# Strassen's method for the layer-1 projections of a two-layer streaming encoder step

## The chip, the cores and the metric

The kernel runs on one core of one Trainium2 chip. The metric is device time in microseconds (us) for one execution of the whole program. The engines are named as in the profile: PE is TensorE with its matmuls (PEld are its weight loads), DVE is VectorE, ACT is ScalarE, POOL is GpSimd, and SP is SyncE, which here issues the DMAs. SBUF is the on-chip memory, PSUM the accumulation memory that PE writes.

## The reference, cut to what matters

A model of two layers (width 1024) takes 512 prompt rows and 32 sample rows. The kernel handles them together as T = 544 columns of a transposed activation matrix. Layer 0 is RWKV-7 time mixing, layer 1 differential attention. The change concerns the input projection of layer 1, its gating, and the output projection that follows:

```python
def diff_layer(x, mk, mv, k_past, v_past, layer_idx, norm_w, w_out, w_in, ...):
    h = rmsnorm(x, norm_w)
    q, k, v, qm, gate = jnp.split(h @ w_in, [MIX_W, 2 * MIX_W, 3 * MIX_W, 3 * MIX_W + MEM_W], axis=-1)
    ...                                     # 12 heads of 128: softmax(q1 k1) - lam * softmax(q2 k2), times v
    y_mem = mem_attention(qm, mk, mv)       # 4 heads of 128 over 256 memory rows
    out = jnp.concatenate([o.reshape(B, T, MIX_W).astype(x.dtype), y_mem], axis=-1) * jax.nn.silu(gate)
    return x + out @ w_out, k, v
```

`w_in` has 1024 rows and 7168 columns: 12 blocks of 128 columns each for q, k and v, 4 for qm and 16 for the gate, 56 blocks in all. All data is float32.

## The kernel before

**Precision scheme.** PE multiplies in a reduced format (`F32R`). Every operand is therefore held as a high part and a low part (`hh`, `hl` for the activations, `whi`, `wlo` for the weights), and a product is three matmuls: high by high, high by low, low by high.

**A projection.** `proj` (L244) computes one block of 128 output columns for all 544 columns. `weights` (L216) loads the block in two halves of 128 x 512 (`raw`, five buffers, L206), casts each half on ACT (L224, `whi`) and subtracts on DVE (L225, `wlo`). Each of `whi` and `wlo` has two buffers that hold a whole block. `gemm` (L228) then runs, for each half of 272 columns, 8 steps over the contraction with three matmuls each (L239 to L241), 48 matmuls in all, into one of the three PSUM banks of `psg`. The caller's `evac` takes the result out of PSUM.

**Order.** The program is written with a tile framework that orders the instructions of each engine ahead of time from priorities and an estimate of durations, and puts in all semaphores. At run time each engine works through its list in order, so an instruction that waits holds up all those behind it.

**Layer 1** (`layer1` L1038, `diff_group` L1111, `mem_head` L782) goes through three groups of four heads. Each head has three projections, k, q and v, whose evacuations write `k`, `qp` (L1141, L1142) and `v`. POOL makes the low part `kz` of the keys (L1152), and the attention of the head follows: score matmuls (L1185 to L1187), maximum on DVE (L776), exponential on ACT (L777), `combine` on DVE (L1250 to L1252), transposes and the product with v (L1193, L1198). After the four heads come the 32 sample rows of the group, and four gate projections (`gate`, L682), each multiplied with the head's output into a tile `og` of SBUF (L1244). Two memory heads follow each of the first two groups, with a projection for qm, attention and a projection for the gate. PE's list mixes the projections of the next head with the attention of the present one.

**Before and after layer 1.** `w_out` (L847) of layer 0 loads sixteen gated tiles from DRAM (`os`, L856), splits each into `hi` and `lo` (L858, L859) and multiplies with the output weights. Its sum `x1` stays in SBUF. The norm of layer 1 scales it into `hn` (L1031), ACT casts `hh` (L1033) and POOL subtracts `hl` (L1034), while PE computes memory values (`mem_kv`, L747). `w_out` of layer 1 finds its sixteen gated tiles `og` in SBUF, splits them, and adds into `x1` (L1097) before the last norm.

Of the kernel before, what the change touches and what calls it, by code (L numbers as in the profile page):

```python
# [8 lines left out]
F32 = mybir.dt.float32  # L9
# [4 lines left out]
ALU = mybir.AluOpType  # L14
# [31 lines left out]
OSB = 4  # L46
ANCH = ('endd',)
# [8 lines left out]
class Trunk:  # L56
# [187 lines left out]
    def proj(self, src, c0, evac):  # L244
        self.gemm([self.weights(src, c0)], [(self.hh, self.hl)], evac)

# [447 lines left out]
    def dest(self, g, sg):  # L694

        return self.o1[g] if self.o1 else sg

    def put(self, g, t):
        if not self.o1:
            self.nc.sync.dma_start(self.oscr[g // 8][:, g % 8, :], t[:])  # L700
# [81 lines left out]
    def mem_head(self, i, h, w, cq, cg, p):  # L782
# [16 lines left out]
        self.proj(w, cq + h * P, lambda ps, v: nc.scalar.mul(q[:, v], ps, P ** -0.5))  # L799
# [37 lines left out]
        sg = self.gate(w, cg + h * P, self.gp)  # L837
        g = self.dest(12 + h, sg)
        for c0, n, val in ((0, TP, mv), (TP, TS, cv)):
            po = self.psg.tile([P, 512], F32, tag="g", name="ps_mo")  # L840
            for j in range(2):
                nc.tensor.matmul(po[:, :n], val[:, j, :], pT[:, j, c0 : c0 + n], start=j == 0, stop=j == 1)  # L842
            nc.vector.scalar_tensor_tensor(g[:, c0 : c0 + n], sg[:, c0 : c0 + n], 0.5, po[:, :n], ALU.mult, ALU.mult)
# [3 lines left out]
    def w_out(self, i, p, order, consume, extra=None):  # L847

        nc = self.nc
        o = {}  # L850
        for g in order:
            if self.o1:
                t = self.o1[g]
            else:
                t = p.tile([P, T], F32, tag="os", name="os", bufs=OSB)
                nc.sync.dma_start(t[:], self.oscr[g // 8][:, g % 8, :])  # L856
            o[g] = hi, lo = [p.tile([P, T], F32R, name=f"{n}{g}") for n in ("hi", "lo")]
            nc.scalar.copy(hi[:], t[:])  # L858
            nc.vector.tensor_tensor(lo[:], t[:], hi[:].bitcast(F32), ALU.subtract)  # L859
        w = self.a["w_out"][i]  # L860
        for k in range(KT):
            ps = [self.psg.tile([P, 512], F32, tag="g", name="ps_g") for _ in range(2)]
            for q in range(2):
                hi, lo = self.weights(w[q * D : (q + 1) * D, :], k * P)
                gs = [g for g in order if g // 8 == q]
                for s in range(2):
                    v = slice(s * TH, s * TH + TH)
                    out = ps[s][:, :TH]
                    for j, g in enumerate(gs):
                        end = q == 1 and j == 7 and extra is None  # L870
                        wh, wl = hi[:, g % 8, :], lo[:, g % 8, :]
                        nc.tensor.matmul(out, wh, o[g][0][:, v], start=q == 0 and j == 0, stop=False)  # L872
                        nc.tensor.matmul(out, wh, o[g][1][:, v], start=False, stop=False)  # L873
                        nc.tensor.matmul(out, wl, o[g][0][:, v], start=False, stop=end)  # L874
                    if q == 1:
                        if extra is not None:
                            extra(k, out, s)
                        consume(k, out, v)
# [26 lines left out]
    def layer0(self, mem):  # L905
# [3 lines left out]
        self.o1 = None  # L909
# [81 lines left out]
        self.x1 = self.pool("x1", 1).tile([P, KT, T], F32, name="x1")  # L991
        with ExitStack() as ctx:
            p = self.pool("wo0", 1, ctx=ctx)
# [20 lines left out]
            def consume(k, ps, v):  # L1014
                nc.scalar.copy(self.x1[:, k, v], ps)
                self.square_sums((k, ps, v), p, sums)

            self.w_out(0, p, range(16), consume, residual)
# [9 lines left out]
            for k in range(KT):  # L1028
                h = p.tile([P, T], F32, tag="os", name="hn", bufs=OSB)
                for q, c, n in ((0, 0, TP), (1, TP, TS)):  # L1030
                    nc.vector.scalar_tensor_tensor(h[:, c : c + n], self.x1[:, k, c : c + n], self.nw[1][:, k : k + 1],  # L1031
                                                   pr[q][:, :n], ALU.mult, ALU.mult)
                nc.scalar.copy(self.hh[:, k, :], h[:])  # L1033
                nc.gpsimd.tensor_tensor(self.hl[:, k, :], h[:], self.hh[:, k, :].bitcast(F32), ALU.subtract)  # L1034
            self.mem_kv(1, mh, ml, (1,), self.psm, "m")
        mctx.close()

    def layer1(self):  # L1038
        nc, a, o = self.nc, self.a, self.o
        w = a["df_in"][0]  # L1040
        op = self.pool("o1", 1)
        self.o1 = [op.tile([P, T], F32, name=f"og{g}") for g in range(16)]
        with ExitStack() as ctx:
            with ExitStack() as c2:
                p = self.pool("df", 1, ctx=c2)
                mp = self.pool("mem1a", 1, ctx=c2)
# [20 lines left out]
                self.kz = [p.tile([P, 2, T], F32R, name=f"kz{i}") for i in range(2)]  # L1067
# [8 lines left out]
        with ExitStack() as ctx:  # L1076
            po = self.pool("wo1", 1, ctx=ctx)
            self.hctx.close()
            p = self.pool("fin", 1, ctx=ctx, side="right")
# [6 lines left out]
            def transposed(s, pool, tag):  # L1086

                for i in range(5):
                    ps = pool[i].tile([P, 512], F32, tag=tag[i], name="ps_f")
                    for k in range(4):  # L1090
                        c = min(i * P, T - P)
                        nc.tensor.transpose(ps[:, k * P : k * P + P], self.x1[:, 4 * s + k, c : c + P], self.ident[:])
                    yield i, slice(P - rows[i], P), ps

            def consume(k, ps, v):
                x = self.x1[:, k, v]
                nc.vector.tensor_tensor(x, ps, x, ALU.add)  # L1097
                self.square_sums((k, x, v), p, sums)
# [4 lines left out]
            self.w_out(1, po, list(range(8)) + [12, 13, 14, 15, 8, 9, 10, 11], consume)  # L1103
# [7 lines left out]
    def diff_group(self, hg, w, p, nlam, sel, neg):  # L1111
# [15 lines left out]
        for j in range(4):  # L1127
            h = 4 * hg + j

            qs = p.tile([P, TS], F32, tag="qs", name="qs", bufs=2)  # L1130
            qp = p.tile([P, 2, T], F32R, tag="qp", name="qp", bufs=QB)
            kh = p.tile([P, 2, T], F32R, tag="kh", name="kh", bufs=QB)
            kz = self.kz[h % 2]
# [4 lines left out]
            def q_parts(ps, c):  # L1138
                for m in range(2):
                    hi = qp[rows[m], m, c]  # L1140
                    nc.scalar.mul(hi, ps[rows[m], :], 0.125)  # L1141
                    nc.vector.scalar_tensor_tensor(qp[rows[1 - m], m, c], ps[rows[m], :], 0.125, hi.bitcast(F32),  # L1142
                                                   ALU.mult, ALU.subtract)
                if c.start:
                    nc.scalar.mul(qs[:], ps[:, TH - TS :], 0.125)

            self.proj(w, MIXW + h * P, lambda ps, c: nc.scalar.copy(k[:, c], ps))
# [5 lines left out]
            self.proj(w, h * P, q_parts)  # L1153
            self.proj(w, 2 * MIXW + h * P, lambda ps, c: nc.scalar.copy(v[:, c], ps))
# [81 lines left out]
        for j in range(4):  # L1236
# [5 lines left out]
            sg = self.gate(w, 3 * MIXW + 512 + (4 * hg + j) * P, self.gp)  # L1242
            g = self.dest(4 * hg + j, sg)
            nc.vector.scalar_tensor_tensor(g[:, :TP], ps[:], self.subs, sg[:, :TP], ALU.mult, ALU.mult)  # L1244
            nc.vector.tensor_tensor(g[:, TP:], oT[:, 32 * j : 32 * j + 32], sg[:, TP:], ALU.mult)
# [8 lines left out]
    def run(self):  # L1254
# [25 lines left out]
        self.layer1()  # L1280

# [33 lines left out]
```

## Time and profile before

| | |
|---|---|
| median of three runs | 1648.49 us (1641.93 to 1654.76) |
| the profiled execution | 1646.78 us, its span 1645.0 us |
| mean granted PE clock | 0.958 |
| PE, DVE, ACT, POOL busy over the span | 93%, 57%, 48%, 24% |
| layer 1 from its first head to the last gate | about 1030 to 1525 us of the span |

The profile has a page with busy shares, a row of the granted PE clock in 40 slices, and the costliest groups of instructions by line of the kernel. The trace behind it answers further views: groups by line in a stretch of time, waits (who waited for whom), a timeline, one line's instructions with their shortest, median and longest duration, and windows (busy time of each engine in given stretches). In a row of the windows, the first pair is the stretch in us from the span's start, then follow its length, the busy time of PE, PEld, DVE, ACT and POOL with the count of instructions of each, the granted PE clock, the DMA engines' busy share and GB/s. In a row of groups, the figures behind the bar are busy us, mean ns of one, and the engine's idle time ahead of them with its cause.

### The profile page before, as it was taken

The numbers are of one execution on the slowest core, as the hardware profiler recorded it, in microseconds if no ns is written. First come the engines' busy times: TensorE is split into PE (matmuls) and PEld (weight loads), VectorE is DVE, ScalarE is ACT, GpSimd is POOL, SyncE is SP. The second block draws the span as 40 slices with busy tenths as digits, with TensorE's granted clock in tenths as the row PEclk, the third lists the DMA queues.
The fourth block names the chain that finished last, engine by engine and source line by source line (L and its number), as shares of the span: only waits on it lengthen the run. The fifth ranks groups of instructions, "written<-read, shape, count | busy, mean of one in ns | idle before, by whom it ended". The sixth has DMA issues, their size and how long they took to land. (4 is left out here: it accounts for less than half of the span.)

```text
span 1645.0 us, 32394 instructions
## 1 busy us (share of the span) xinstructions
PE 1537.7 (93%) x12112; PEld 1399.9 (85%) x12112; DVE 941.0 (57%) x2452; ACT 786.1 (48%) x2075; POOL 387.6 (24%) x936
## 2 busy tenths in 40 slices
PE   6996998899999899988998999999999999999997
PEld 6985887788888788877887998899999999999997
DVE  7651766774886587574666225446535464456543
ACT  7542464364455356434445224556346544564422
POOL 2050642651653464364000003100001000010000
PEclk9995999997999999996999999999999999999999
DMA  6422122212222212223226433522232222322222
GB/s 210 125 84 50 53 63 49 66 56 49 60 68 64 59 57 64 56 50 105 67 74 207 136 101 103 139 85 80 84 111 78 83 80 80 96 78 70 90 78 75
DMA packets 265383, 139.23 MB, mean 85 GB/s; under 512 B 56505, under 2 KB 255426, under 8 KB 265226
## 3 DMA queue, kind: packets, MB, share of 16 engines
q1 hardware_dynamic: 265226, 137.15, 29.4%
q8 instruction: 96, 1.57, 0.4%
q14 instruction: 61, 0.50, 0.1%
HBM read 110.98 MB, written 22.78 MB: 81 GB/s over the span
## 5 line engine op out<-in xcount | busy, mean ns | idle before, releaser
L239 PE MATMUL ps_g<-hh,whi 128*128 128x272 f32 x1808 | 550.7, 305 | 0.2
L240 PE MATMUL ps_g<-hl,whi 128*128 128x272 f32 x1808 | 550.2, 304 | 0.0
L241 PE MATMUL ps_g<-hh,wlo 128*128 128x272 f32 x1808 | 543.9, 301 | 0.5 <-DVE wlo L225 0.5
L225 DVE TENSOR_TENSOR wlo<-raw,whi 128x512 fp32r<-128x512 f32 x322 | 223.0, 706 | 256.6 <-ACT whi L224 251.8
L239 PEld LDWEIGHTS ps_g<-hh,whi 128*128 128x128 f32 x1808 | 349.9, 194 | 4.4 <-issue 1.3
L240 PEld LDWEIGHTS ps_g<-hl,whi 128*128 128x128 f32 x1808 | 349.2, 193 | 4.1
L241 PEld LDWEIGHTS ps_g<-hh,wlo 128*128 128x128 f32 x1808 | 348.6, 193 | 3.9 <-DVE wlo L225 1.2
L224 ACT CAST whi<-raw 128x512 fp32r<-128x512 f32 x322 | 195.3, 619 | 265.9 <-PE ps_g L240 130.2
L540 POOL TENSOR_TENSOR tm<-u,m 102x84 f32<-102x84 f32 (+23 forms) x372 | 153.9, 414 | 179.1 <-DMA m<-sc 152.0
L542 POOL TENSOR_TENSOR u<-u,tm 102x84 f32<-102x84 f32 (+23 forms) x372 | 157.4, 423 | 27.5
L872 PE MATMUL ps_g<-hi,whi 128*128 128x272 f32 x512 | 150.2, 294 | 8.6 <-ACT whi L224 6.7
L873 PE MATMUL ps_g<-lo,whi 128*128 128x272 f32 x512 | 148.8, 291 | 1.2 <-DVE lo L859 1.2
L874 PE MATMUL ps_g<-hi,wlo 128*128 128x272 f32 x512 | 148.9, 291 | 0.0
L1152 POOL TENSOR_TENSOR kz<-k,kh 64x544 fp32r<-64x544 f32 x24 | 32.6, 1357 | 418.4 <-ACT kh L1150 417.4
L872 PEld LDWEIGHTS ps_g<-hi,whi 128*128 128x128 f32 x512 | 98.0, 191 | 9.1 <-ACT whi L224 6.9
L873 PEld LDWEIGHTS ps_g<-lo,whi 128*128 128x128 f32 x512 | 97.7, 191 | 1.9 <-DVE lo L859 1.9
L874 PEld LDWEIGHTS ps_g<-hi,wlo 128*128 128x128 f32 x512 | 97.7, 191 | 0.0
L639 DVE SCALAR_TENSOR_TENSOR SB<-ps_c,dl,sd 64x64 f32<-64x64 f32 x168 | 47.4, 282 | 37.3 <-PE ps_c L633 35.5
L1034 POOL TENSOR_TENSOR hl<-hn,hh 128x544 fp32r<-128x544 f32 x8 | 11.9, 1519 | 229.9 <-ACT hh L1033 229.9
L341 ACT COPY raw<-ps_g 128x272 f32<-128x272 f32 x74 | 28.5, 386 | 73.9 <-PE ps_g L241 49.9
L777 ACT ACTIVATE pt<-ps_s,snm 128x128 f32<-128x128 f32 (+3 forms) x96 | 50.7, 530 | 22.4 <-DVE snm L776 22.0
L628 ACT COPY yt<-ps_c 64x128 f32<-64x128 f32 x96 | 24.9, 259 | 69.5 <-DVE avz L627 68.8
(397 smaller groups left out, 2768.0 us busy)
## 6 DMA issues: line engine op xcount, KB each, us to landing
raw<-in_rw_in_dram SPq DMA_DIRECT2D x114, 256.0 KB
raw<-in_df_in_dram SPq DMA_DIRECT2D x112, 256.0 KB
raw<-in_w_out_dram SPq DMA_DIRECT2D x64, 256.0 KB
m<-sc SPq DMA_DIRECT2D x36, 136.0 KB
oscr<-sg SPq DMA_DIRECT2D x16, 272.0 KB
os<-oscr SPq DMA_DIRECT2D x16, 272.0 KB
raw<-in_w_mem_k_dram SPq DMA_DIRECT2D x16, 256.0 KB
raw<-in_w_mem_v_dram SPq DMA_DIRECT2D x16, 256.0 KB
```

The lines of the kernel that those rows point to most:

```text
L224: nc.scalar.copy(hi[:, k], raw[q][:])
L225: nc.vector.tensor_tensor(lo[:, k], raw[q][:], hi[:, k].bitcast(F32), ALU.subtract)
L239: self.mms.append(nc.tensor.matmul(out, hi[:, k, :], xh[:, k, v], start=(b == 0 and k == 0), stop=False))
L240: self.mms.append(nc.tensor.matmul(out, hi[:, k, :], xl[:, k, v], start=False, stop=False))
L241: self.mms.append(nc.tensor.matmul(out, lo[:, k, :], xh[:, k, v], start=False, stop=(b == n - 1 and k == KT - 1)))
L540: nc.gpsimd.tensor_tensor(tm[:, :n, :wd], u3[:, :n, kx : kx + 1].to_broadcast(sh), m3[:, kx : kx + 1, kx + 1 :].to_broadcast(sh), ALU.mult)
L542: nc.gpsimd.tensor_tensor(u3[:, :n, kx + 1 :], u3[:, :n, kx + 1 :], tm[:, :n, :wd], ALU.add)
L639: self.last = nc.vector.scalar_tensor_tensor(Snew[hc, hc], ps[hc, 2, hc], d, sd[hc, hc], ALU.mult, ALU.add)
L777: nc.scalar.activation(pt[:rows, m, :n], ps[m], AF.Exp, bias=nm[:rows, m : m + 1], accum_out=rs[:rows, m : m + 1])
L872: nc.tensor.matmul(out, wh, o[g][0][:, v], start=q == 0 and j == 0, stop=False)
L873: nc.tensor.matmul(out, wh, o[g][1][:, v], start=False, stop=False)
L874: nc.tensor.matmul(out, wl, o[g][0][:, v], start=False, stop=end)
```

## The change

Two blocks of 128 columns are computed together by seven products of half the contraction (4 of the 8 steps) and half the columns (272) in place of the eight that two `proj` calls need. This is the Winograd form of Strassen's method. A new function `pair` (with `unit`) takes the place of `proj` in layer 1; layer 0 keeps `proj`. The 56 blocks become 28 pairs: k with v for each head (12), q of two heads (6), gates of two heads (6), qm with gate for each memory head (4).

```diff
+    def unit(self, raw, t, half):
+        k = slice(half * KT // 2, (half + 1) * KT // 2)
+        self.nc.scalar.copy(t[0][:, k], raw[:])
+        self.nc.vector.tensor_tensor(t[1][:, k], raw[:], t[0][:, k].bitcast(F32), ALU.subtract)
+
+    def pair(self, src, c0, c1, o0, o1):
...
+        def parts():
+            return [self.wp.tile([P, KT, P], F32R, tag=g, name=g, bufs=2) for g in ("whi", "wlo")]
+
+        def product(t, half, x):
...
+        a11, a12 = load(self.wp, "raw", RAWS, 0, c0), load(self.wp, "raw", RAWS, 1, c0)
+        a21, a22 = load(self.ws, "ra", 2, 0, c1), load(self.wp, "raw", RAWS, 1, c1)
+        s1 = self.ws.tile([P, n, P], F32, tag="rs", name="rs1", bufs=2)
+        t = parts()
+        self.unit(a11, t, 0)
+        self.unit(a12, t, 1)
+        nc.gpsimd.tensor_tensor(s1[:], a21[:], a22[:], ALU.add)
+        nc.gpsimd.tensor_tensor(a21[:], a11[:], a21[:], ALU.subtract)
+        nc.gpsimd.tensor_tensor(a11[:], s1[:], a11[:], ALU.subtract)
+        nc.gpsimd.tensor_tensor(a12[:], a12[:], a11[:], ALU.subtract)
+        u = [self.ws.tile([P, TH], F32, tag=f"u{i}", name=f"u{i}", bufs=1) for i in range(3)]
+        ps = product(t, 0, at(0, L))
+        nc.scalar.copy(u[0][:], ps)
+        ps = product(t, 1, at(n, L))
+        nc.vector.tensor_tensor(o0[:, L], ps, u[0][:], ALU.add)
+        t = parts()
+        self.unit(a11, t, 0)
+        self.unit(s1, t, 1)
+        ps = product(t, 0, ax(0))
+        nc.vector.tensor_tensor(u[1][:], ps, u[0][:], ALU.add)
+        ps = product(t, 1, at(0, R))
+        nc.vector.tensor_tensor(u[2][:], ps, u[1][:], ALU.add)
+        t = parts()
+        self.unit(a21, t, 0)
+        self.unit(a12, t, 1)
+        ps = product(t, 0, ax(1))
+        nc.vector.tensor_tensor(o1[:, R], ps, u[2][:], ALU.add)
+        nc.vector.tensor_tensor(u[1][:], ps, u[1][:], ALU.add)
+        ps = product(t, 1, at(n, R))
+        nc.vector.tensor_tensor(o0[:, R], ps, u[2][:], ALU.add)
+        t = parts()
+        self.unit(a22, t, 0)
+        ps = product(t, 0, ax(2))
+        nc.vector.tensor_tensor(o1[:, L], ps, u[1][:], ALU.add)
```

The callers take whole results of 544 columns out of SBUF tiles (`results`, two buffers) in place of evacuating halves from PSUM; `gate_of` applies the gate function to such a result.

```diff
-            self.proj(w, MIXW + h * P, lambda ps, c: nc.scalar.copy(k[:, c], ps))
+            self.pair(w, MIXW + h * P, 2 * MIXW + h * P, k, v)
...
-            self.proj(w, h * P, q_parts)
-            self.proj(w, 2 * MIXW + h * P, lambda ps, c: nc.scalar.copy(v[:, c], ps))
+            if j % 2 == 0:
+                x, two = self.results(), []
+                self.pair(w, h * P, h * P + P, *x)
...
-            sg = self.gate(w, 3 * MIXW + 512 + (4 * hg + j) * P, self.gp)
-            g = self.dest(4 * hg + j, sg)
+            if j % 2 == 0:
+                x, c = self.results(), 3 * MIXW + 512 + (4 * hg + j) * P
+                self.pair(w, c, c + P, *x)
+            g = self.gate_of(x[j % 2])
...
+            self.put(4 * hg + j, g)
```

The activations need sums of their quarters too. They are made at the norm between the layers, in place in `x1`, and kept in `hx`; `x1` itself goes to DRAM (`xscr`) before, and its SBUF tile is then used by `kz` and `kh`:

```diff
+                if v.start:
+                    nc.sync.dma_start(self.xscr[:, k, :], x1[:, k, :])
...
+            for k in (0, 4, 1, 5, 2, 6, 3, 7):
...
+                v = L if k < half else slice(0, T)
+                split(nc.gpsimd, self.hh[:, k, v], self.hl[:, k, v], x1[:, k, v])
+            for k in range(half):
+                t = p.tile([P, 3, TH], F32, tag="tt", name="tt", bufs=2)
...
+                nc.gpsimd.tensor_tensor(t[:, 1], b22, b12, ALU.subtract)
+                nc.vector.tensor_tensor(b12, b12, b11, ALU.subtract)
+                nc.vector.tensor_tensor(t[:, 0], b22, b12, ALU.subtract)
+                nc.vector.tensor_tensor(t[:, 2], b21, t[:, 0], ALU.subtract)
+                split(nc.vector, self.hx[0][:, k], self.hx[1][:, k], t[:])
+                split(nc.vector, self.hh[:, k, R], self.hl[:, k, R], b12)
```

The sixteen gated tiles of layer 1 go to DRAM and come back through three buffers (`gated`, split out of `w_out`), groups 0 to 2 after the second group of heads, the other thirteen behind the last; `x1` is loaded back for the last sum:

```diff
+                    if hg == 1:
+                        mctx.close()
+                        pe = self.pool("wo1e", 1, ctx=ctx, side="right")
+                        self.gated(pe, EARLY, x, pe, 3)
+            order = list(range(8)) + [12, 13, 14, 15, 8, 9, 10, 11]
             po = self.pool("wo1", 1, ctx=ctx)
-            self.hctx.close()
-            p = self.pool("fin", 1, ctx=ctx, side="right")
+            self.gated(po, [g for g in order if g not in EARLY], x, pe, 3)
+            p = self.pool("fin", 1, ctx=ctx)
+            x1 = p.tile([P, KT, T], F32, name="x1b")
+            nc.sync.dma_start(x1[:], self.xscr[:])
```

138 lines of the change are left out of this document (87 added, 51 removed).

## The prediction

> **What bounds the kernel now.** The page comes first, for the span, then the windows view over layer 1, because the change is worth what that stage makes of it.
>
> ```profile
> span 1645.0 us, 32394 instructions
> ...
> core 0: us, PE busy (x) PEld busy (x) DVE busy (x) ACT busy (x) POOL busy (x), PEclk, DMA share, GB/s
> 1030.00:1525.00 495.00, 488.05 (x3744) 450.88 (x3743) 262.25 (x720) 263.03 (x764) 32.58 (x24) 1.00 0.31 89
> 950.00:975.00 25.00, 25.00 (x205) 25.00 (x204) 6.55 (x12) 6.41 (x14) 0.00 (x0) 1.00 0.32 95
> 525.00:550.00 25.00, 24.35 (x171) 20.86 (x170) 24.04 (x65) 10.35 (x30) 21.79 (x49) 1.00 0.27 78
> 575.00:650.00 75.00, 72.14 (x613) 64.42 (x610) 58.03 (x169) 43.72 (x115) 38.78 (x96) 1.00 0.22 62
> ```
>
> In the first row, layer 1, PE is busy for 488 of 495 us at full clock: PE is the bound, DVE is half busy (262 us), ACT too (263 us), POOL nearly idle (33 us). The second row, dense matmuls of 272 columns, gives the pitch: 25.00 / 205 = 0.122 us. The last two show how full DVE gets anywhere in this trace: 96% over 25 us, 77% over 75 us. They are needed below. Next, the groups by line within layer 1 say what DVE does there, and two rows from the whole program serve as prices:
>
> ```profile
> L225 DVE TENSOR_TENSOR wlo<-raw,whi 128x512 fp32r<-128x512 f32 x110 | 75.7, 690 | 143.2 <-ACT whi L224 142.3
> L224 ACT CAST whi<-raw 128x512 fp32r<-128x512 f32 x110 | 68.0, 618 | 100.0 <-PE ps_g L240 81.9 <-issue 17.9
> L1142 DVE SCALAR_TENSOR_TENSOR qp<-ps_g,qp 64x272 fp32r<-64x272 f32 x48 | 21.1, 439 | 25.2 <-ACT qp L1141 24.4
> L689 DVE SCALAR_TENSOR_TENSOR sg<-sg,ps_g 128x272 f32<-128x272 f32 x31 | 13.3, 430 | 4.1 <-ACT sg L688 4.1
> L1152 POOL TENSOR_TENSOR kz<-k,kh 64x544 fp32r<-64x544 f32 x24 | 32.6, 1357 | 418.4 <-ACT kh L1150 417.4
> ...
> L1097 DVE TENSOR_TENSOR x<-ps_g,x x16: 441/442/444, 1542.2 to 1631.7; 128x272 f32<-128x272 f32 x16
> L859 DVE TENSOR_TENSOR lo<-os,hi 128x544 fp32r<-128x544 f32 x16 | 11.4, 725 | 10.1 <-ACT hi L858 10.0
> ```
>
> DVE waits 142 us for casts that wait for PE to free a weight buffer (82 us): today DVE has time to lose.
>
> **What the change removes from PE.** 56 projections of 48 matmuls are 2688, 28 pairs of 7 x 4 x 3 = 84 are 2352: 336 fewer, 336 x 0.122 = 41 us. If PE stayed as full as now, layer 1 would take 495 - 41 = 454 us.
>
> **What it adds to DVE.** Weight halves to split: 4 per pair before, 7 after. They are formed after the sums, so nothing is shared: 196 x 0.690 = 135.2 in place of 75.7 us. Seven additions per pair of a PSUM product to an SBUF tile, the shape of L1097: 196 x 0.442 = 86.6 us, where the old evacuations of k and v were ACT's. The q parts become 24 of 64x544, priced like L859: 24 x 0.725 = 17.4 for 21.1. The gates become 16 of 544 columns: 11.6 for 13.3. In sum 262.3 - 75.7 + 135.2 + 86.6 - 3.7 - 1.7 = 403 us of DVE work. Against 454 us that is 89%. ACT gains 3 casts per pair, 84 x 0.618 = 52 us, and sheds part of its evacuations: at most 315 us, no bound.
>
> **What it adds to POOL, and to DVE through POOL.** Four 128x512 additions per pair, 112 in all, each about 1.36 x 512/544 = 1.28 us (estimate from L1152 and the row of five below), 143 us beside the 33 for `kz`. POOL has room. But at the norm between the layers the trace shows what happens when POOL and DVE both run operations with two SBUF inputs. The two rows of L1034 are POOL without and with DVE's splits beside it; the two of L225 are DVE's splits in that stretch and, for comparison, over layer 0:
>
> ```profile
> L1034 POOL TENSOR_TENSOR hl<-hn,hh x5: 1338/1360/1365, 1014.6 to 1020.2; 128x544 fp32r<-128x544 f32 x5
> L1034 POOL TENSOR_TENSOR hl<-hn,hh x4: 1338/1792/1798, 1020.2 to 1025.0; 128x544 fp32r<-128x544 f32 x4
> L225 DVE TENSOR_TENSOR wlo<-raw,whi x4: 990/1829/1837, 1021.1 to 1025.5; 128x512 fp32r<-128x512 f32 x4
> L225 DVE TENSOR_TENSOR wlo<-raw,whi x82: 667/683/966, 168.2 to 759.5; 128x512 fp32r<-128x512 f32 x82
> ...
> L1031 DVE SCALAR_TENSOR_TENSOR hn<-x,PB,ps_r x14: 241/496/748, 1013.8 to 1020.9; 128x512 f32<-128x512 f32 x7, 128x32 f32<-128x32 f32 x7
> ```
>
> A split takes 1.83 us instead of 0.68: it stands behind the POOL addition, and POOL behind it (1.79 for 1.36). So one POOL addition can cost DVE 1.15 us. An operation that reads PSUM for one input is not held: L1031 shows at most 0.748 us beside the same POOL work. The Trainium skill, in "SBUF — State Buffer", section "Who interferes with whom", says the same as a rule: a pair of ports is shared, locked for the whole instruction, and the second to issue blocks; it speaks against this change, and the four rows agree. By that rule at its fullest, 1.28 us for each of 136 POOL additions, layer 1 would take (403 + 174) / 0.95 = 607 us and the time would be 1772 us.
>
> How much of 1.15 us falls due per POOL addition, call it b, the trace does not show for a DVE this dense. Lower bound 0: the 24 `kz` of layer 1 ran at 1.357 us, unheld, beside a half idle DVE. Upper bound 1.15, which would make (403 + 156) / 0.95 = 589 us of the stage and 1753 us of the time. The third addition starts when the split of `a11` ends, with the split of `a12` next in DVE's list: a full hold. Elsewhere an addition from PSUM (0.44 us) comes first about half the time, which leaves 0.7, and sometimes DVE is waiting anyway. I take b = 0.65, nearer to the row of 1.83, over 136 POOL additions: 88 us. DVE's demand becomes 403 + 88 = 491 us. That exceeds PE's 454 and nearly fills today's 495. DVE turns into the bound.
>
> Behind a held split stand, in DVE's order, the additions that free the three `psg` banks (a product lasts 12 x 0.122 = 1.46 us, so two spare banks cover 2.9 us) and the maxima L776 of the softmax; PE waits for both. How full can DVE be over 500 us? Between the rows of 0.77 and 0.96 I take 0.95, since in layer 1 there is work of several heads to choose from throughout. 491 / 0.95 = 517 us, 22 more than before.
>
> **The norm between the layers.** The first row is from the timeline; the next two are waits of PE that are there today, and in the window beside them the clock is down:
>
> ```profile
> 1026.80 0.36 ACT L756 COPY memx<-ps_g 128x256 f32<-128x256 f32 x1
> ...
> PE ps_ckT L1121 <- DMA ck<-in_cache_k_dram: 2.6, 1, 2.6
> PE ps_g L241 <- DVE wlo L225: 1.9, 1, 1.9
> ...
> 1013.00:1030.00 17.00, 13.96 (x99) 13.10 (x98) 14.54 (x27) 9.77 (x21) 14.10 (x12) 0.90 0.51 147
> ```
>
> POOL's `hl` work stays about the same (four of 272 columns are halved, four subtractions are added), then the first pair puts three additions ahead of its third product: 8 x 1.36 + 3 x 1.28 = 14.7 us from 1014.6, and with ten holds of 0.43 us (1.79 - 1.36) it ends near 1034. PE has its memory values and two products until about 1027, where today's last memory value is evacuated (first row above). DVE gets four times three subtractions of 272 columns and two splits, about 11 us, all of the kind that is held. I put the loss at 7 us: 1034 - 1027. Bounds: -1 (the additions of the pair slip ahead, today's 1.9 us wait goes) and 12 (the clock falls as well).
>
> **The end of layer 1.** Sixteen writes and sixteen loads of 272 KB, and 2.2 MB of `x1` out and back. Most lies under layer 1 (DMA share 0.31). Thirteen groups come back through three buffers, and the tiles of groups 7 and later lie where `hx` was, free only after PE's last product. Layer 0's `w_out` starts from DRAM in the same way, layer 1's from SBUF; the waits of PE at these two starts are, in this order:
>
> ```profile
> PE ps_g L872 <- ACT whi L224: 6.7, 1, 6.7
> ...
> PE ps_g L872 <- ACT hi L858: 1.9, 1, 1.9
> PE ps_g L873 <- DVE lo L859: 1.2, 1, 1.2
> ```
>
> 6.7 against 3.1: +4 us. Bounds 0 (groups 0 to 6 are ready and cover the rest) and 10 (the load of `x1`, last in SP's queue, comes late for L1097, and PE has no free bank).
>
> **Sum.** 22 + 7 + 4 = 33 us on the profiled execution's 1646.8 (span 1645.0): 1680. That execution lies 1.7 us below the median of the runs, so 1682 us on the median's scale.
>
> **Rivals.** One per cent of the time (16 us) is about what a measurement of this kernel can tell from no change.
>
> *PE stays the bound (faster).* If the order puts POOL's additions beside score maxima and PSUM additions, b is near 0, DVE needs 403 us, and 403 / 0.89 fits in PE's 454. For it: PE's list mixes heads already, and L1152 was never held. Against: 89% must hold for 450 us, where 77% is the most over 75 us. It decides when b stays under about 0.2. Time: 1648.5 - 41 + 11 = 1618 us, somewhat more if PE loses a few per cent. Chance 0.18.
>
> *Gain and holds cancel (same).* b = 0.45: 403 + 61 = 464, / 0.95 = 489, 6 less than today, with the 11 of both ends: 1653 us. For it: the sign of the body flips only at b = 0.5. Chance 0.22.
>
> *Two weight buffers starve PE (slower still).* The seventh product stands alone in its buffer, so the next pair's first weights have 1.46 us to come: cast 0.62 and split 0.69 fit, a held split (1.83) is 1.0 late. The third product waits for the POOL sum, cast and split in a row: 1.28 + 0.62 + 0.69 = 2.6 within the 2.93 of two products, but held 1.69 + 0.62 + 1.83 = 4.1, 1.2 late. 28 x 2.2 = 62 us if attention fills none of it, and PE loses clock in stretches like the one of 0.90 above: 454 / 0.95 + 62 = 540, 45 more, with both ends 1705 us and up. Against: 160 us of attention matmuls are there to fill the holes. Chance 0.14.
>
> The forecast itself has 0.46.
>
> **How the numbers follow.** Faster 0.18, within 1% 0.22, slower 0.46 + 0.14 = 0.60. The forecast's own range is 1665 to 1710 (b from 0.53 to 0.85). For eight in ten I leave out the faster half of the first rival and the far end of the third: 1630 to 1722, the upper end being b = 0.92 with the same ends.
>
> **What would show it.** In the profile after: 2352 matmuls of pairs, 336 fewer, at an unchanged pitch; L225's successor 196 times in layer 1 with a mean above 0.69 us, towards 1.1, and many near 1.8; POOL additions at 1.3 to 1.8 us; DVE over 90% busy there, PE under 90%; PE's waits on weight splits and on free banks. Right on the mechanism, wrong on the size, if those durations are long but the stage is short. It is wrong if the splits stay at 0.69, if PE is over 97% busy in layer 1, or if the stage is shorter than 480 us.

## The result and the profile after

| | before | after |
|---|---|---|
| median | 1645.21 us (1630.5 to 1654.76, 4 runs) | 1700.33 us (1698.62 to 1703.1, 4 runs) |
| ratio | | 1.0345 (95%: 1.0264 to 1.0426) |
| profiled execution, span | 1645.0 us | 1699.4 us |

The changed kernel is 3.4% slower. The row of engines of the profile's page (busy time, share of the span, instructions), before and then after, has the 336 matmuls fewer, and a fuller DVE and POOL:

```profile
PE 1537.7 (93%) x12112; PEld 1399.9 (85%) x12112; DVE 941.0 (57%) x2452; ACT 786.1 (48%) x2075; POOL 387.6 (24%) x936
...
PE 1533.5 (90%) x11776; PEld 1370.0 (81%) x11776; DVE 1144.5 (67%) x2712; ACT 827.2 (49%) x2103; POOL 552.7 (33%) x1052
```

To see where the 54.4 us of span came from, both traces are cut at the same instructions of PE: the last matmul of layer 0's `w_out`, the first transposes of each group (`ps_ckT`), the first product of each group's sample rows (`ps_os`), and the first and last matmul of layer 1's `w_out`. A group's heads lie between `ps_ckT` and `ps_os`; its gates and the two memory heads between `ps_os` and the next `ps_ckT`, called the memory stretch below. The windows view of layer 1, cut so, before the change:

```profile
1039.60:1153.00 113.40, 112.04 (x853) 102.82 (x853) 60.38 (x158) 67.58 (x201) 8.12 (x6) 0.98 0.33 92
1153.00:1208.30 55.30, 55.19 (x411) 50.88 (x412) 29.86 (x88) 21.97 (x62) 0.00 (x0) 1.00 0.28 80
1208.30:1330.70 122.40, 121.04 (x938) 111.82 (x937) 63.55 (x165) 71.36 (x209) 10.86 (x8) 1.00 0.32 92
...
sum 489.80, PE 483.59 PEld 446.39 DVE 260.97 ACT 261.21 POOL 29.85; mean PE 80.60 PEld 74.40 DVE 43.49 ACT 43.54 POOL 4.97
```

and after it:

```profile
1041.80:1157.60 115.80, 108.46 (x793) 95.48 (x793) 102.20 (x211) 75.06 (x207) 46.64 (x32) 0.99 0.33 94
1157.60:1229.40 71.80, 57.70 (x358) 48.01 (x358) 55.71 (x119) 29.22 (x68) 23.41 (x16) 0.88 0.27 83
1229.40:1355.70 126.30, 118.41 (x872) 105.51 (x871) 107.76 (x221) 77.61 (x211) 46.81 (x32) 0.99 0.32 90
...
sum 529.30, PE 476.82 PEld 416.32 DVE 448.29 ACT 297.95 POOL 188.90; mean PE 79.47 PEld 69.39 DVE 74.72 ACT 49.66 POOL 31.48
```

Before, PE is busy for 121.0 of 122.4 us of a group's heads. After, it has less to do (872 instructions for 938), yet the heads take 3.9 us longer, with DVE at 107.8 us in place of 63.6. The largest loss, 16.5 us each time, is in the two memory stretches, where DVE has only 55.7 of 71.8 us and the granted clock is 0.88. By groups, DVE and then POOL in layer 1 after the change:

```profile
L252 DVE TENSOR_TENSOR wlo<-raw,whi 128x512 fp32r<-128x512 f32 x135 | 120.9, 910 | 10.3 <-ACT whi L251 8.3
L252 DVE TENSOR_TENSOR wlo<-rs,whi 128x512 fp32r<-128x512 f32 x27 | 33.8, 1252 | 0.0
L1369 DVE TENSOR_SCALAR pt<-pt,srs 128x128 f32<-128x128 f32 (+4 forms) x51 | 25.1, 492 | 0.2
L1368 DVE TENSOR_TENSOR srs<-srs,ls 128x1 f32<-128x1 f32 x51 | 15.1, 296 | 0.4
```

```profile
L289 POOL TENSOR_TENSOR raw<-raw 128x512 f32<-128x512 f32 x27 | 42.4, 1569 | 3.5 <-POOL raw L288 2.1
L1254 POOL TENSOR_TENSOR kx<-k,kx 64x544 fp32r<-64x544 f32 x24 | 36.6, 1527 | 38.3 <-ACT kx L1252 37.4
```

The splits have gone from 0.69 to a mean of 0.91 and 1.25 us. The view of this one line (shortest, median and longest duration in ns) shows that the mean is made of two kinds:

```profile
L252 DVE TENSOR_TENSOR wlo<-raw,whi x140: 664/686/2724, 1027.6 to 1567.4; 128x512 fp32r<-128x512 f32 x140
...
L252 DVE TENSOR_TENSOR wlo<-rs,whi x28: 677/1391/1777, 1029.8 to 1560.1; 128x512 fp32r<-128x512 f32 x28
```

Most splits of `raw` run beside no POOL instruction; of all 196 splits, 51 took over 1.0 us and 25 over 1.7, and each of the 51 ran beside one. The two stretches around layer 1 grew as well: the norm between the layers from 34.4 to 45.7 us, `w_out` of layer 1 from 102.3 to 115.1 us. PE's waits in the one and in the other:

```profile
PE ps_g L242 <- DVE wlo L226: 12.7, 1, 12.7
...
PE ps_g L949 <- ACT hi L931: 4.5, 4, 1.9
PE ps_g L950 <- DVE lo L932: 3.4, 4, 2.6
```

So, in us of the profiled executions: layer 1 +39.5, the norm +11.3, `w_out` +12.8, and layer 0 -9.1. The last is scatter: all kernels of this study have the same instructions up to the end of layer 0's `w_out`, and yet this end lies at 1005.2 us in the kernel before, at 993.2 in e9, a variant of it, and from 991.6 to 998.9 in the kernels with the change (e1 apart). That is why the experiments, which the next section describes, are read by stage, each from one execution. Medians and ratios below leave out slow runs, those over 1.5% above the fastest of their kernel; e1's profiled execution is one of these (granted clock 0.936, against 0.946 after the change), but what it loses lies ahead of its norm, which starts at 1014.8 us, and the granted clock of its layer 1 is 0.96 as after the change.

| us | norm | heads of the three groups | memory stretches | last gates | layer 1 | `w_out` 1 |
|---|---|---|---|---|---|---|
| before | 34.4 | 113.4, 122.4, 122.4 | 55.3, 55.3 | 21.0 | 489.8 | 102.3 |
| after | 45.7 | 115.8, 126.3, 125.5 | 71.8, 71.8 | 18.1 | 529.3 | 115.1 |
| e1 sums aside | 47.0 | 117.2, 126.4, 125.3 | 69.4, 67.3 | 16.4 | 522.0 | 114.7 |
| e2 no sums | 41.8 | 112.0, 117.6, 117.8 | 63.2, 63.3 | 16.4 | 490.3 | 115.3 |
| e3 sums on DVE | 41.7 | 115.5, 125.0, 124.3 | 69.8, 65.7 | 19.6 | 519.9 | 113.2 |
| e4 plain memory heads | 45.4 | 115.9, 125.7, 129.1 | 56.6, 56.5 | 18.1 | 501.9 | 114.6 |
| e5 covers | 46.1 | 118.1, 126.3, 124.9 | 58.1, 58.2 | 20.2 | 505.8 | 107.9 |
| e6 covers, sums on DVE | 39.5 | 117.3, 125.2, 125.6 | 56.6, 56.3 | 21.7 | 502.7 | 107.4 |
| e7 as e6, some of DVE's work moved to ACT | 39.5 | 111.6, 118.5, 117.6 | 52.7, 52.9 | 19.6 | 472.9 | 105.3 |
| e8 covers, no sums | 41.8 | 107.4, 117.3, 117.3 | 50.1, 50.1 | 18.5 | 460.7 | 106.1 |
| e9 before, the same work moved to ACT | 35.1 | 112.7, 121.6, 121.6 | 55.8, 55.7 | 21.5 | 488.9 | 102.3 |
| e10 as e7, sums on POOL | 46.1 | 110.4, 119.7, 119.6 | 56.4, 56.5 | 19.3 | 481.9 | 107.4 |

### The profile page after: what moved, and what is told of

The parts are those of the page before. It is cut to its first block, busy times and chain, and to the rows that moved or that the text cites. A ratio compares the mean times of both kernels' runs of the same rounds, so it can differ in the third digit from the quotient of the medians.

```text
span 1699.4 us, 32494 instructions
## 1 busy us (share of the span) xinstructions
PE 1533.5 (90%) x11776; PEld 1370.0 (81%) x11776; DVE 1144.5 (67%) x2712; ACT 827.2 (49%) x2103; POOL 552.7 (33%) x1052
## 4 chain that ended last, share of the span: by engine, by line
PE 49%; DVE 17%; POOL 11%; DMA 8%; ACT 7%; issue 5%; SPq 3%; DVEq 0%; POOLq 0%; ACTq 0%
POOL u L610 5%; POOL tm L608 5%; DVE wlo L252 4%; PE ps_p L274 4%; PE ps_g L949 4%; PE ps_g L950 3%; PE ps_g L951 3%; PE ps_p L272 3%; PE ps_p L273 3%; PE ps_g L241 3%; PE ps_g L240 3%; PE ps_g L242 3%; DMA m<-sc 2%; PE ps_mo L919 2%; PE ps_o L1313 2%
## 5 line engine op out<-in xcount | busy, mean ns | idle before, releaser
L241 PE MATMUL ps_g<-hl,whi 128*128 128x272 f32 x912 | 286.0, 314 | 0.0
L240 PE MATMUL ps_g<-hh,whi 128*128 128x272 f32 x912 | 279.7, 307 | 0.1
L242 PE MATMUL ps_g<-hh,wlo 128*128 128x272 f32 x912 | 279.6, 307 | 0.2 <-DVE wlo L226 0.2
L241 PEld LDWEIGHTS ps_g<-hl,whi 128*128 128x128 f32 x912 | 178.8, 196 | 3.9
L240 PEld LDWEIGHTS ps_g<-hh,whi 128*128 128x128 f32 x912 | 178.8, 196 | 2.8 <-issue 0.7
L242 PEld LDWEIGHTS ps_g<-hh,wlo 128*128 128x128 f32 x912 | 178.8, 196 | 2.7 <-DVE wlo L226 0.5
L949 PE MATMUL ps_g<-hi,whi 128*128 128x272 f32 x512 | 151.3, 298 | 8.2 <-ACT hi L931 4.5
L950 PE MATMUL ps_g<-lo,whi 128*128 128x272 f32 x512 | 150.8, 295 | 3.4 <-DVE lo L932 3.4
L274 PE MATMUL ps_p<-hh,wlo 128*128 128x272 f32 x448 | 137.0, 306 | 0.8 <-DVE wlo L252 0.8
L272 PE MATMUL ps_p<-hh,whi 128*128 128x272 f32 x448 | 135.8, 303 | 0.5 <-ACT whi L251 0.4
L252 DVE TENSOR_TENSOR wlo<-raw,whi 128x512 fp32r<-128x512 f32 x140 | 125.3, 910 | 12.2 <-ACT whi L251 10.2
L273 PE MATMUL ps_p<-hl,whi 128*128 128x272 f32 x448 | 132.7, 296 | 0.0
L949 PEld LDWEIGHTS ps_g<-hi,whi 128*128 128x128 f32 x512 | 98.8, 194 | 9.8 <-ACT hi L931 5.7
L274 PE MATMUL ps_p<-hxh,wlo 128*128 128x272 f32 x336 | 101.1, 301 | 3.0 <-DVE wlo L252 2.9
L950 PEld LDWEIGHTS ps_g<-lo,whi 128*128 128x128 f32 x512 | 99.3, 194 | 4.7 <-DVE lo L932 4.7
L288 POOL TENSOR_TENSOR raw<-rs,raw 128x512 f32<-128x512 f32 x28 | 41.8, 1494 | 185.0 <-DVE wlo L252 157.8
```

The source lines that it names most:

```text
L240: self.mms.append(nc.tensor.matmul(out, hi[:, k, :], xh[:, k, v], start=(b == 0 and k == 0), stop=False))
L241: self.mms.append(nc.tensor.matmul(out, hi[:, k, :], xl[:, k, v], start=False, stop=False))
L242: self.mms.append(nc.tensor.matmul(out, lo[:, k, :], xh[:, k, v], start=False, stop=(b == n - 1 and k == KT - 1)))
L252: self.nc.vector.tensor_tensor(t[1][:, k], raw[:], t[0][:, k].bitcast(F32), ALU.subtract)
L272: nc.tensor.matmul(out, t[0][:, w, :], x[0](k), start=k == 0, stop=False)
L273: nc.tensor.matmul(out, t[0][:, w, :], x[1](k), start=False, stop=False)
```

## The experiments

Three theories were set against each other. *Holds*: POOL's additions lengthen DVE's operations, and DVE's list bounds layer 1. *Chain*: the products wait for POOL's sums themselves, four in series. *Lost cover*: a memory head's pair now makes qm and gate ahead of the scores, so that the gate's products no longer lie beside its softmax.

**e1, sums aside.**

```diff
+        d = [self.ws.tile([P, n, P], F32, tag="rs", name="rs1", bufs=2) for _ in range(2)]
-        nc.gpsimd.tensor_tensor(s1[:], a21[:], a22[:], ALU.add)
-        nc.gpsimd.tensor_tensor(a21[:], a11[:], a21[:], ALU.subtract)
+        nc.gpsimd.tensor_tensor(d[0][:], a21[:], a22[:], ALU.add)
+        nc.gpsimd.tensor_tensor(d[1][:], a11[:], a21[:], ALU.subtract)
...
-        self.unit(s1, t, 1)
+        self.unit(a22, t, 1)
```

> The four POOL additions of every pair are issued as before, on the same operands, but write to two tiles that nothing reads; the products take the raw quarters in place of the sums (so the sums are left out of the result). POOL's work and DVE's splits stay, no split waits for POOL's sums any more. Holds (DVE's splits stand behind POOL's instructions, wherever their data come from): the splits of the pair stay at a mean of 0.9 us and more, and the time stays within 10 us of the changed kernel, 1690 to 1705. Chain (the products wait for four POOL additions in series, some 6 us a pair): 1650 to 1670, with the splits still at 0.9. Lost cover (the memory heads' pair takes q and gate ahead of the softmax, so nothing covers it): no answer here, the two stretches from a group's end to the next group stay at 72 us each.

Measured: 1693.53 us, ratio to the kernel before 1.0295 (1.0195 to 1.0395). Layer 1 fell by 7.3 us only, with the splits of `raw` at 0.834 us, a little under the 0.9 expected:

```profile
L252 DVE TENSOR_TENSOR wlo<-raw,whi 128x512 fp32r<-128x512 f32 x162 | 132.2, 834 | 13.8 <-ACT whi L251 12.2
```

DVE's busy time in layer 1 fell too, from 448.3 to 432.6 us, so the 7.3 us need not be the chain's alone. The products' wait for the sums is a small part: the chain theory is out as the main cause.

**e2, no sums.** The four additions are deleted, and `s1` is `a22` as in e1.

> The four POOL additions of every pair are left out, and the raw quarters are multiplied in their place (so the sums are left out of the result); all loads, splits, products and additions from PSUM stay. Holds: the splits go back to 0.69 us, DVE loses about 84 us of held time, and layer 1 falls from 529 us to 460 to 475: 1630 to 1650. Chain: the same time as with the additions set aside, 1650 to 1670. Lost cover: the heads gain, the two stretches with memory heads stay at 68 to 72 us (55.3 before the change), and the time stays above 1655.

Measured: 1659.67 us, 1.0098 (1.0068 to 1.0128). Layer 1 fell by 39.0 us, to what it took before the change. DVE's groups there, to be read against those after the change:

```profile
L252 DVE TENSOR_TENSOR wlo<-raw,whi 128x512 fp32r<-128x512 f32 x163 | 116.5, 733 | 13.2 <-ACT whi L251 11.0
L1364 DVE TENSOR_SCALAR pt<-pt,srs 128x128 f32<-128x128 f32 (+4 forms) x51 | 19.1, 374 | 0.2
L1363 DVE TENSOR_TENSOR srs<-srs,ls 128x1 f32<-128x1 f32 x51 | 7.7, 151 | 0.4
```

And one window of heads and the sum over layer 1:

```profile
1212.10:1329.70 117.60, 114.58 (x871) 103.89 (x871) 89.80 (x221) 77.17 (x211) 12.08 (x8) 1.00 0.34 97
...
1036.90:1527.20 490.30, 465.47 (x3393) 414.18 (x3393) 375.63 (x952) 297.12 (x783) 35.72 (x24) 0.97 0.33 97
```

DVE's busy time fell from 448.3 to 375.6 us: 72.7 us, or 0.65 us for each of the 112 additions, is what POOL's sums cost DVE. Without them PE is the bound of the heads again (114.6 of 117.6 us). Layer 1 came out above the 460 to 475 of pure holds because the memory stretches stayed at 63 us, 15.9 us above before in sum; they also fell below the 68 to 72 that lost cover alone was to leave. Both causes are there, and they overlap.

**e3, sums on DVE.** `nc.gpsimd` becomes `nc.vector` in the four additions.

> The four sums of a pair are made by DVE instead of POOL: 112 more DVE instructions at about 0.69 us, 77 us, and no hold but from the subtraction of kz. Holds: about 84 us of held time are exchanged for 77 us of work, so the time stays at 1685 to 1705. Chain: the series takes 2.8 us instead of some 6 us and the sums come earlier: 1665 to 1680. If DVE's list is the bound and a hold costs less than the work (DVE is often idle when held), slower: 1705 to 1730.

Measured: 1685.27 us, 1.0257 (1.0178 to 1.0335), at the lower edge of what holds were to give. Layer 1 fell by 9.4 us and the norm by 4.0. The window of layer 1:

```profile
1036.30:1556.20 519.90, 471.01 (x3395) 417.59 (x3395) 451.83 (x1060) 296.91 (x783) 39.19 (x24) 0.97 0.32 92
```

DVE is busy for 451.8 us, against 448.3 after the change: it exchanges its holds for about as much work, as the hold theory has it; the norm, which holds only the first pair's sums, gains in each of the kernels without POOL's sums (39.5 to 41.8 us, against 45.4 to 47.0 with them).

**e4, plain memory heads.**

```diff
-            x = self.results()
-            self.pair(w, cq + h * P, cg + h * P, *x)
-            nc.scalar.mul(q[:], x[0][:], P ** -0.5)
-            g = self.gate_of(x[1])
+        self.proj(w, cq + h * P, lambda ps, v: nc.scalar.mul(q[:, v], ps, P ** -0.5))
...
+        g = self.gate(w, cg + h * P, self.gp)
```

> Layer 1's four memory heads make q by a plain projection ahead of the scores and the gate by another after them, as before the change (their operand's right half holds differences for the first four steps, so their values are others); every other pair stays. Lost cover: the two stretches from a group's end to the next group go from 71.8 us to 55 to 60 each, the time to 1668 to 1680. Holds: only 16 POOL additions fewer, at 0.62 us, 10 us: 1688 to 1695, with the stretches at 66 or more. Chain: four series fewer of some 28: 1688 to 1697.

Measured: 1674.25 us, 1.0174 (1.011 to 1.0238). The memory stretches fell from 71.8 to 56.6 and 56.5 us although PE has 24 matmuls more to do in each. What was lost with the cover is seen in these rows: the two largest waits of PE in the memory stretches after the change (one of its weight loads, one of its matmuls),

```profile
PEld ps_mt L905 <- ACT mp L894: 16.1, 4, 4.2
...
PE ps_mt L905 <- DVE mrs L895: 14.6, 4, 3.9
```

the group of the product of the memory values there,

```profile
L919 PE MATMUL ps_mo<-mpT,mhv 128*128 128x512 f32 x16 | 15.9, 1099 | 2.7 <-ACT mpT L907 2.7
```

against the same wait of PE in all of e4's layer 1,

```profile
PE ps_mt L899 <- DVE mrs L889: 2.1, 2, 1.1
```

the same product there,

```profile
L912 PE MATMUL ps_mo<-mpT,mhv 128*128 128x512 f32 x16 | 7.5, 592 | 0.0
```

and the window of e4's first memory stretch:

```profile
1158.50:1215.10 56.60, 52.96 (x383) 47.38 (x382) 39.30 (x99) 24.97 (x64) 7.79 (x6) 1.00 0.33 100
```

After the change PE's matmuls stand still until the softmax is through, up to 3.9 us at a time (its weight loads up to 4.2); the granted clock of the stretch falls to 0.88, and the same product takes 1.10 instead of 0.59 us. From 1200 to 1205 us, where the first of these products run, the granted clock is 0.50. With the gate's matmuls beside the softmax the clock of the stretch is 1.00. The Trainium skill, in "TensorE: Matmul & The Clock Gate", part 1 on the HAM clock gate, puts an idle window of about 3.4 us ahead of a halved clock; waits of 3.9 and 4.2 us and a product at nearly twice its time agree with it. But e4 also takes work from DVE in each stretch (39.3 us busy, against 55.7), so it can't tell alone how much the cover is worth; e5 can.

**e5, covers.** Three edits at once, in stages of their own (the main lines, with comments added):

```diff
-            self.pair(w, cq + h * P, cg + h * P, *x)          # per memory head
+        for c in (cq, cg):                                    # per two memory heads
+            x = self.results()
+            self.pair(w, c + hs[0] * P, c + hs[1] * P, *x)
+            for s, y in zip(st, x):
+                s.send(y)                                     # after cq: scores, softmax; after cg: gate, output
...
+            self.mem_kv(1, mh, ml, (1,), self.psm, "m")
             for k in range(half):
                 t = p.tile([P, 3, TH], F32, tag="tt", name="tt", bufs=2)
...
-EARLY = (0, 1, 2)
+EARLY = (0, 1, 2, 3, 4, 5, 6, 7, 12, 13, 14)                 # fetched as they are, split at w_out
...
-            nc.sync.dma_start(x1[:], self.xscr[:])
+                if k < KT - 1 and not v.start:
+                    nc.sync.dma_start(x1[:, k + 1, :], self.xscr[:, k + 1, :])
```

> Three edits of the changed kernel, each in a stretch of its own; POOL keeps its sums. (1) The memory heads of a group are paired otherwise: qm of both as one pair, then the scores of both, then the gates of both as one pair, so that a pair's products lie beside the softmax. (2) The last memory values (mem_kv) come ahead of the forming of the Strassen operands in the norm between the layers. (3) Eleven of the sixteen gated tiles are fetched during the third group as they are, x1 comes back in eight pieces along the output blocks. Lost cover: the two stretches from a group's end to the next group go from 71.8 us to 56 to 62 each; norm placement: from 45.7 us to 37 to 41; tail: from 128.3 us to 116 to 120; together 1655 to 1668, the heads unchanged at 116 to 126. If holds and not the missing cover make the stretches long, these stay above 66 us; if the transfers as such (and not when they come) make the tail long, it stays above 125.

Measured: 1670.49 us, 1.0175 (1.0125 to 1.0226), above the 1655 to 1668 expected. The first memory stretch:

```profile
1163.10:1221.20 58.10, 50.84 (x359) 44.55 (x358) 53.96 (x116) 28.53 (x68) 20.13 (x14) 1.00 0.31 91
```

The memory stretches came to 58 us as expected. The pairs and POOL's sums are still there and DVE is busy for 54.0 us, nearly as after the change, and yet 27.3 of the 33.0 us that the two stretches had lost come back, with the granted clock at 1.00: the place of the products is the cause. `w_out` gained 7.2 us, to 121 on the scale of the expectation, which counts to the end of the span: a little less than expected. The norm did not gain (46.1 us): the wait of 12.7 us for `mem_kv`'s weights went, and others came in its place, the longest 5.4 us for `memx`.

**e6, covers and sums on DVE.**

> The kernel with the three edits, and the four sums of a pair on DVE in place of POOL. Holds: 8 to 12 us below the kernel with the three edits alone, as the sums on DVE took 9 us from layer 1 without them; heads 115 to 125, stretches with memory heads 55 to 60; 1640 to 1655. If the covers bring back what the order of DVE's list cost, the two gains overlap and the time is within 4 us of the three edits alone.

Measured: 1663.55 us, 1.0135 (1.009 to 1.018), above the 1640 to 1655 expected, as e5 was above its own. The gain over e5 was 6.9 us between the medians, between the 8 to 12 us expected of holds and the 4 at most of overlapping gains; the stages show 6.6 in the norm and 3.1 in layer 1.

**e7, covers, sums on DVE, relief to ACT.** As e6, and three of DVE's operations in the heads move to ACT (the relief):

```diff
-        nc.vector.tensor_scalar(pt[:, 1, :n], pt[:, 1, :n], rs[:, 1:2], None, ALU.mult)
+        nc.scalar.mul(pt[:, 1, :n], pt[:, 1, :n], rs[:, 1:2])
...
-                nc.vector.tensor_copy(ot[:, t, :], po[:, :P])
+                nc.scalar.copy(ot[:, t, :], po[:, :P])
...
-                nc.vector.tensor_scalar(on[j][:, t, :], on[j][:, t, :], ss[:, 2, 4 * j + t : 4 * j + t + 1], None, ALU.mult)
+                nc.scalar.mul(on[j][:, t, :], on[j][:, t, :], ss[:, 2, 4 * j + t : 4 * j + t + 1])
```

> The three edits, the sums on DVE, and three of DVE's operations in the heads moved to ACT (the scaling of the second map in combine, the copy of ot, the scaling of ot at the group's end), some 45 us of DVE's work in layer 1. DVE's list is the bound of the heads: they fall from 125 to 117 to 120 us each, as without sums, and layer 1 to 470 to 482; 1622 to 1640, below the kernel before. ACT's list becomes the wait (PE's scores wait for the exponentials): heads at 122 us and more, layer 1 above 488; 1645 to 1660.

Measured: 1631.59 us, 0.9945 (0.9916 to 0.9975): 4% below the changed kernel and 0.5% below the kernel before, less than the one per cent that the prediction took for the limit of a measurement. The window of the second group's heads and layer 1 as a whole, in e6 and then in e7:

```profile
1211.10:1336.30 125.20, 116.82 (x872) 105.54 (x871) 110.25 (x247) 76.36 (x210) 13.18 (x8) 0.99 0.33 93
...
1037.20:1539.90 502.70, 465.20 (x3409) 416.57 (x3408) 448.48 (x1061) 296.67 (x785) 38.91 (x24) 0.99 0.33 96
```

```profile
1197.70:1316.20 118.50, 114.68 (x876) 105.42 (x879) 102.52 (x215) 86.79 (x242) 12.75 (x8) 0.99 0.36 101
...
1033.40:1506.30 472.90, 456.08 (x3410) 411.36 (x3408) 415.09 (x914) 341.87 (x932) 37.89 (x24) 1.00 0.35 102
```

DVE lost 33.4 us of work (45 had been expected), layer 1 lost 29.8 us, and PE is busy for 114.7 of 118.5 us of the heads. ACT took over 45 us without becoming a bound. DVE's list was the bound of the heads.

**e8, covers and no sums** (e5 and e2 together).

> The three edits, and the four sums left out (the raw quarters are multiplied in their place, so the sums are left out of the result): what the change could give at most with sums that cost nothing. Heads at 112, 118 and 118 us, the stretches with memory heads at 53 to 56, layer 1 at 470 to 476, against 490 before the change: 1620 to 1640. If the fewer matmuls carry the whole predicted 41 us, layer 1 is at 450 or less.

Measured: 1620.55 us, 0.9889 (0.9841 to 0.9937).

```profile
1033.40:1494.10 460.70, 448.28 (x3375) 404.51 (x3375) 372.41 (x949) 295.58 (x783) 35.91 (x24) 1.00 0.35 104
```

With sums that cost nothing and the covers in place, layer 1 gains 29.1 us on the kernel before, some 10 more than expected, in the memory stretches (50.1 us each) and in the first group's heads (107.4). PE's busy time is 35.3 us under that of before, not 41; no run took apart why.

**e9, the kernel before with e7's three moves to ACT, and nothing else.**

> The kernel before the change, with the same three operations of the heads moved from DVE to ACT and nothing else. If PE bounds it (its share in the heads is 98 to 99%), this changes nothing: within 5 us of the kernel before, layer 1 at 488 to 493 us; then the gain of the kernel with covers, sums on DVE and relief belongs to the fewer matmuls. If the relief shortens chains that PE waits for, 8 us or more below the kernel before, and that gain is the relief's.

Measured: 1635.29 us, 0.9981 (0.9953 to 1.001); layer 1 at 488.9 us.

```profile
1028.30:1517.20 488.90, 483.05 (x3707) 446.33 (x3707) 227.92 (x570) 307.45 (x907) 31.95 (x22) 1.00 0.30 87
```

DVE has 33 us less to do and layer 1 is 0.9 us shorter: PE bounded the kernel before. What e7 gains in layer 1 (488.9 to 472.9) therefore belongs to the change together with its repairs. Over the whole program part of it is lost again, as e7's norm and `w_out` are 4.4 and 3.0 us longer than e9's: the medians are 3.7 us apart and the intervals of the two ratios overlap, so it is not shown that the repaired change beats the kernel before with the same work moved.

**e10, as e7 with the sums on POOL.**

> The three edits and the three operations moved from DVE to ACT, with the sums back on POOL: beside the same kernel with the sums on DVE (layer 1 473 us) it tells what POOL's sums cost once DVE has room. Holds as an amount of DVE's time: some 76 us of held time against 77 us of work, so the same within 5 us, layer 1 at 470 to 480, the norm between the layers 5 us longer, 1632 to 1643. Holds that strike where PE waits next (the splits of the running pair): layer 1 at 485 to 495, 1645 to 1660.

Measured: 1640.28 us, 1.0012 (0.9982 to 1.0041). The time is the one expected of holds as an amount of DVE's time; layer 1 at 481.9 us is 2 us over its range and 9.0 us over e7's, where at most 5 had been expected: the heads are within 2 us of e7's, the memory stretches 3.7 us longer each, the norm 6.6. Against e5, with the same holds, layer 1 lost 23.9 us by the relief alone. So a hold costs more time where DVE has no room: POOL's sums cost layer 1 45.1 us in the full list (e5 against e8) and 21.2 with the relief (e10 against e8). The second figure may be too low, since e8 has no relief.

## Why the prediction was right, and where it was not

The forecast, slower by way of DVE, was right, and 1700.33 us lies in its range, 18 us above the 1682 named. That it came so near is in part luck: with the cover restored (e5) layer 1 is 16.0 us longer than before, less than the 22 predicted, and only a cause that the prediction does not have brings it to 39.5. Step by step:

*The price of a hold* was right. Predicted b = 0.65 us; measured 72.7 us over the pairs' 112 additions, 0.65 us. The prediction put the same price on the 24 `kz`; no run leaves these out, and an estimate from e2's splits (mean 0.733, median 0.684 us), 163 x 0.049 = 8 us, makes it less there, some 0.33 us for each. The Trainium skill's rule ("SBUF — State Buffer", section "Who interferes with whom"), at its fullest, gave layer 1 607 us by the prediction's estimate, against 529 measured: the lock is seen in 51 long splits, but most splits (median 0.686 us) met no POOL addition. The additions from PSUM were not held, as predicted: the longest of all 196 after the change took 0.444 us, and the longest of the 61 that ran beside POOL 0.443. One of their rows:

```profile
L301 DVE TENSOR_TENSOR u<-ps_p,u 128x272 f32<-128x272 f32 x27 | 11.7, 433 | 3.2 <-PE ps_p L274 2.6
```

*DVE's demand without holds* was too high: 403 us, where e2 shows 376. The term set durations on top of a busy time; in the trace of before, the groups of layer 1 add up to 286 us where the window has DVE busy for 261, since one instruction's time overlaps the next's. The work itself was counted rightly: 286 and the 141 us that the sum adds are 427, and e2's groups add up to 424.

*The fill of 0.95 was the step that failed.* DVE was busy for 448 of 529 us, 0.85, and for 0.88 of layer 1 in e5, with the cover back. The last two errors worked against each other: 491 / 0.95 = 517 was predicted, 448 / 0.85 = 529 measured. In the heads DVE was at 0.85 to 0.92 with PE at 0.93 to 0.94 (after, e3, e6), and the reason given, work of several heads to choose from throughout, does not hold in the memory stretches, where one softmax follows its own head's products. There DVE reached 0.78 and PE 0.80.

*How PE comes to wait* was half right. The prediction has PE wait for free `psg` banks and for the softmax behind its maxima. The view of PE's waits in layer 1 after the change lists none for a free `psg` bank. Outside the memory stretches the longest are these two, for the exponentials and for POOL's low part of the keys (`kx` is the new name of the tile of `kz`),

```profile
PE ps_s L1300 <- ACT pt L848: 9.0, 12, 2.1
...
PE ps_s L1301 <- POOL kx L1254: 5.1, 6, 1.5
```

and in e2, without the sums, the first is

```profile
PE ps_s L1295 <- ACT pt L843: 4.4, 12, 0.4
```

and the second is gone. POOL's sums thus also reach PE through POOL's own list, a path that the prediction does not have.

*The lost cover is missing from the prediction.* It priced the memory heads' pairs by count alone and not by the place of the gate's products, which the pairing of qm with gate shows. e5 returns 27.3 of the 33 us that the two stretches lost, e4 30.5. (In e2 the same stretches keep 16 of the 33: the two causes overlap, and are not simply added.)

*The norm*: +7 predicted, +11.3 measured, inside its bounds. POOL's sums of the first pair, which the prediction had as the cause, are 4 to 7 us of it (e2 and e3 against after, e7 against e10). The long wait that shows is another than the one named: 12.7 us of `mem_kv` for a weight split on DVE, and when e5 took it away, others came and the norm stayed at 46.1. The rest, 4 to 7 us, would lie with the forming of the operands on DVE; no run took these apart.

*The end of layer 1*: +4 predicted, +12.8 measured, over its upper bound of 10. The row of layer 0's start did not price it. PE's busy time and clock dip in the first two windows of `w_out` after the change:

```profile
1571.10:1591.00 19.90, 15.14 (x84) 13.90 (x83) 11.02 (x20) 7.89 (x14) 0.00 (x0) 0.74 0.86 303
1591.00:1611.00 20.00, 16.60 (x107) 15.07 (x107) 8.30 (x14) 6.23 (x12) 0.00 (x0) 0.91 0.45 136
```

In the first the DMA engines are 86% busy at 303 GB/s and the clock is 0.74. PE's waits in both are nearly all for the splits of the gated tiles (the rows of L949 and L950 above); for an addition into `x1`, which the prediction feared for its upper bound, it waits 0.3 us only. Whether the load of `x1` delays the tiles is not shown. Earlier fetches and `x1` in pieces returned 7 to 10 us (e5 to e8, e10); which of the two did more stays open.

*The rivals.* "PE stays the bound" did not come about, yet it is where the repaired kernel arrives: e7 and e8 have PE at 0.96 to 0.97 of the heads, with no sums on POOL. "Two weight buffers starve PE" is refuted by the waits of PE's matmuls in layer 1 after the change:

```profile
PE ps_p L274 <- DVE wlo L252: 3.2, 9, 0.5
```

Of what was to be seen, the 336 matmuls, the long splits, the POOL additions (means of 1.33 to 1.57 us) and PE at 90% were there; DVE over 90% and waits for free banks were not.

## What to carry to other kernels

Price a change by the engine that the saved work is shifted to: here 35 us less for PE (e8) cost DVE 187 us with the holds, and layer 1 gains only once DVE has been given room (e7) and each wait has its cover again (e5). Ask of every operation that is moved what its old place was covering. And the highest share an engine reaches over a whole stage is set by the chains in that stage, so take it from the stage's own kind of work rather than from the densest window of the trace.

## What was not expected of the hardware

Not only splits were lengthened beside POOL's work: the scaling in `combine` went from 374 to 492 ns (L1369, against L1364 of e2), and an operation on 128x1 elements from 151 to 296 ns (L1368, against L1363); 10 of its 51 ran beside a POOL instruction and took 889 ns in the mean, the others 151. In the memory stretches, behind waits of about 4 us, a product of 512 columns took 1099 instead of 592 ns.
